# Output projection and feed-forward as 2x2 block products with seven multiplications

## The chip, the core and the metric

The kernel runs on one core of a Trainium2 chip. TensorE multiplies (a stationary operand of 128x128 is loaded, a moving operand of up to 512 columns streams past it, results add up in PSUM banks of 128x512 float32), VectorE and ScalarE work elementwise, GpSimd does little here, and SyncE (SP) issues nearly all DMA. The metric is the device time of one execution in microseconds.

## The reference

One layer of a flow-matching generator over 512 latent tokens of width 2048, with 256 context tokens, in float32. Cut to what matters here:

```python
hx = modulate(rmsnorm(x, norm1_g), sh1, sc1)
q, k, v, g, lf, lb, cb, cc, cx = split_proj(hx @ w_in)
o_x = gla_bidir(...)                       # 4 heads, both directions, from the context's states
y_conv = cb * conv_grid(cc * cx, conv_w)
mix = concat([norm(o_x) * gla_g * silu(g), y_conv]) @ w_out          # [512, 2048] @ [2048, 2048]
x_next = x + gt1 * mix
h2 = modulate(rmsnorm(x_next, norm2_g), sh2, sc2)
x_next = x_next + gt2 * ((silu(h2 @ wg) * (h2 @ wu)) @ wd)           # 2048 -> 2 x 5632 -> 2048
return rmsnorm(x_next, final_g)
```

sh, sc and gt come from `silu(c) @ w_mod + b_mod`.

## The kernel before

Every large product is made from two parts of each operand: `split` casts to a reduced float32 on ScalarE (the high part, L87) and subtracts on VectorE (the low part, L88), and `mm3` adds three matmuls: low x high, high x low, high x high. Activations are kept as [features, tokens]. Weights arrive in units of 128x1024 (512 KB) through four `raw` buffers (`load_w`), and their parts go to three buffers `whi` and three `wlo`. One unit feeds 24 matmuls of 512 columns: its eight 128x128 blocks are the stationary operand, the 512 tokens move, and the result is a tile of 128 features by 512 tokens in one PSUM bank.

The first part projects K, V, q, the gates and the convolution's inputs, and weaves the stages of the attention (`do_gla`) between units of the projections (`weave`). At each step `mod_some` streams 0.7 tiles of the modulation matrix through the same `raw` buffers and reduces each half tile on VectorE (L351): 48 of the 64 tiles run there, 16 beside the first group of the feed-forward.

The output projection then makes 16 tiles of features from the 16 tiles of the mix. The last two go by halves of the tokens, so that the second norm of one half (`row_scale`, `norm2`) runs beside the matmuls of the other. In the feed-forward a group of eight hidden tiles is made (gate `ag` and up `au`, 48 matmuls each; `swiglu`), and then added to all 16 tiles of the output (`acc`, L793); the last group and the final norm go by halves again.

A tile scheduler orders the instructions of each engine ahead of time, by priorities in the order in which the program names them and by its own estimate of when each can run. On the chip every engine works its list off in order, and SP's DMA waits in the same way for free buffers.

Of the kernel before, what the change touches and what calls it, by code (L numbers as in the profile page):

```python
# [13 lines left out]
P = 128  # L14
# [10 lines left out]
NCH = SEQ // CHUNK  # L25
# [3 lines left out]
HT = FFN // P  # L29
EPS = 1e-6  # L30
# [3 lines left out]
# columns of the "cols" input  # L34
C_G1, C_G2, C_FG, C_BMOD, C_GLA, C_CONV = 0, 16, 32, 48, 144, 146
NCOLS = 170
# square constant blocks of the "cst" input
B_ID, B_TRIF, B_TRIB, B_SUFF, B_SUFB, B_MF, B_MB, B_ONE, B_ONE16, B_SELX, B_SELC = range(11)
NBLK = 11
# columns of the "sm" input  # L40
# [5 lines left out]
def tile_hybrid_block(  # L46
    ctx: ExitStack,
    tc: tile.TileContext,
    xT, cT, ccol, crow, cst, sm, cols, gates,
    wsc, wsh, wm2, wk, wv, wl, wq, wg, wc, wo, wfg, wfu, wfd,  # L50
# [7 lines left out]
    xpool = ctx.enter_context(tc.tile_pool(name="xpool", bufs=24))  # L58
    pspool = ctx.enter_context(tc.tile_pool(name="pspool", bufs=1, space=bass.MemoryType.PSUM))

# [29 lines left out]
    def split_scaled(hi, lo, src, scale):  # L90
        """Parts of src * scale, with a scale per partition."""
        nc.scalar.activation(hi, src, AF.Copy, scale=scale)
        nc.vector.scalar_tensor_tensor(lo, src, scale, hi.bitcast(F32), op0=ALU.mult, op1=ALU.subtract)  # L93

    def split_shifted(hi, lo, src, shift):
        """Parts of src + shift, with a shift per partition."""
        nc.scalar.activation(hi, src, AF.Identity, bias=shift)
        nc.vector.scalar_tensor_tensor(lo, src, shift, hi.bitcast(F32), op0=ALU.add, op1=ALU.subtract)  # L98
# [7 lines left out]
    def load_w(src, k, eng=None):  # L106
        """One unit of weights, split into its parts, as [128, k, n]."""
# [14 lines left out]
    def rsqrt_of_sum(pool, s, scale, n):  # L122
        """1 / sqrt(s * scale + eps): square root and reciprocal, then one Newton step."""
# [12 lines left out]
    def row_bcast(ps, pool, r):  # L136
        """ps[m, 128 * tt + t] = r[t, tt] for every m."""
# [6 lines left out]
    cstt = cpool.tile([P, NBLK, P], F32, name="cstt")  # L144
    smt = cpool.tile([P, NSM], F32, name="smt")
    colt = cpool.tile([P, NCOLS], F32, name="colt")
    maskt = cpool.tile([P, 2, SEQ], U8, name="maskt")
    gatet = cpool.tile([33, 2, 512], F32, name="gatet")
    lfT = cpool.tile([33, SEQ + CTX], F32, name="lfT")
# [3 lines left out]
    cbc = cpool.tile([P, D], F32, name="cbc")  # L153
    ident, ones, one16 = cstt[:, B_ID, :], cstt[:, B_ONE, :], cstt[:, B_ONE16, :]
    onecol = cstt[:, B_ONE, 0:1]
# [5 lines left out]
    es_hx = ExitStack()  # L161
    hxpool = es_hx.enter_context(tc.tile_pool(name="hxpool", bufs=1))
# [10 lines left out]
    # Silu of the zeros brings in the table before c is there  # L173
# [3 lines left out]
    def mod_cols(src, c0, n):  # L177
        """silu(c) and silu(c_ctx) times n * 128 columns of w_mod: [128 columns, n, (x, ctx)] in PSUM."""
# [27 lines left out]
    def scaled_chunk(i):  # L206
# [12 lines left out]
        for n, src, acc, dst, pool, q in ((SEQ, xt, saccx, hx, hxpool, 0), (CTX, ct, saccc, hc, hcpool, 1)):  # L219
            hi = pool.tile([P, n], F32R, tag=f"hi{i}", name="hhi")  # L220
            lo = pool.tile([P, n], F32R, tag=f"lo{i}", name="hlo")
# [21 lines left out]

    nc.sync.dma_start(cstt, cst)
# [26 lines left out]
    # ======== V projection of heads 0 and 1 behind the stream of the shift columns ========  # L271
# [6 lines left out]
    def shift_chunk(i):  # L278
        """Chunk i of hx and hc from the scaled rows: norm, then the shift."""
# [21 lines left out]
    def lf_finish(pl, a, n):  # L301
        """Sum of the four partial sums, as rows of lfT."""
# [41 lines left out]
    def mod_some(n, last):  # L344
        """n more of the tiles of 128 features; n may be a fraction."""
# [10 lines left out]

    def mod_finish(a, b):
# [71 lines left out]
    def log_gates(pool, tag, pzs, las):  # L429
        """la = log_sigmoid(z) = min(z, 0) - ln(1 + exp(-|z|)); its 1 / 16 is in the constants."""  # L430
# [8 lines left out]
    def proj_units(acc, wsrc, x, units=(0, 1), part=ALL):  # L439
        """acc = (weight columns)^T x, for one tile of 128 columns; yields after each unit of weights."""  # L440
# [6 lines left out]
    def proj_pair(accs, wsrcs, x, units, part, ws=None, eng=None):  # L447
# [4 lines left out]
        for n, u in enumerate(units):  # L452
            kept = ws is not None and n == 0
            if not kept:
                ws = [load_w(src[u], 8, None if n else eng) for src in wsrcs]
            aw = list(zip(accs, ws))
            for k, (acc, w) in ([(k, a) for a in aw for k in range(8)] if kept else
                                [(k, a) for k in range(8) for a in aw]):
                mm3(acc[:, part], sl(w, ALL, k), sl(x[8 * u + k], ALL, part), n == 0 and k == 0, n == 1 and k == 7)
        return ws  # L460

    def run(*gens):
        for g in gens:
            for _ in g:
                pass

    # ======== context states ========
# [54 lines left out]
    def weave(stages, fill):  # L522
        """A chain's stages between units of the projections, so that TensorE has work while it waits."""
        for _ in stages:
            next(fill, None)
            mod_some(0.7, 48)
        for _ in fill:
            mod_some(0.7, 48)
# [4 lines left out]
    # ======== gated linear attention per head, gated short convolution in between ========  # L533
# [3 lines left out]
    for d in range(2):  # L537
        t = gp.tile([P, SEQ], F32, name=f"msk{d}")
        nc.gpsimd.memset(t, 0.0)
        msk.append(t)  # L540
    las = [[gp.tile([P, 512], F32, name=f"la{d}_{tt}") for tt in range(NX)] for d in range(2)]
# [9 lines left out]
    def do_gla(h):  # L551
        """One head over blocks of 128 tokens; within a block, decays are relative to its middle."""
# [3 lines left out]
        kn = gp.tile([P, 512], F32, tag="kn", name="kn")  # L556
# [3 lines left out]
        for d in range(2):  # L560
# [4 lines left out]
            e = gp.tile([P, 512], F32, tag=f"qe{d}", name="qe")  # L565
            nc.scalar.activation(e, pcm, AF.Exp)
            ke = gp.tile([P, 512], F32, tag="ke", name="ke", bufs=2)
            nc.scalar.activation(ke, pcm, AF.Exp, scale=-1.0)
            # the column of the middle, whose own decay is one, carries the decay from the block's start to it
# [10 lines left out]
            kk = gp.tile([P, 512], F32, tag=f"kd{d}", name="kk")  # L580
# [15 lines left out]
        # o as [tokens, values], two blocks of tokens to a bank  # L596
# [25 lines left out]
        # per-head norm  # L622
# [8 lines left out]
        # back to [values, tokens]; gain and swish gate  # L631
# [35 lines left out]
    mod_some(48, 48)  # L667
    owed[0] = 0.0
    mod_finish(0, 48)
# [3 lines left out]
    es_hx.close()  # L673

    # ======== output projection, gated residual ========
    xnpool = ctx.enter_context(tc.tile_pool(name="xnpool", bufs=1, side="right"))
    mpool = ctx.enter_context(tc.tile_pool(name="mpool", bufs=1))

    def pair(i):
        return (mpool.tile([P, SEQ], F32R, tag=f"hi{i}", name="mhi"),  # L680
                mpool.tile([P, SEQ], F32R, tag=f"lo{i}", name="mlo"))

    order = list(range(8, 16)) + list(range(8))
    mh = [None] * 16
    for i in order:
        mh[i] = pair(i)
        split(*mh[i], mix[i])
    HALF = SEQ // 2
    parts = (slice(0, HALF), slice(HALF, SEQ))
    xn = []  # L690
    sacc = xnpool.tile([P, SEQ], F32, name="sacc")

    def square(m, t, acc):
        """Adds t^2 to acc."""
        s = acc if m == 0 else xnpool.tile([P, SEQ], F32, tag="sqn", name="sqn", bufs=2)[:, : t.shape[-1]]
        nc.scalar.activation(s, t, AF.Square)  # L696
        if m:
            nc.gpsimd.tensor_tensor(acc, acc, s, op=ALU.add)  # L698

    def row_scale(sums):  # L700
        """1 / rms of the rows of one half, the same on every partition; sums: tiles of squares to add up."""
        pms = bank("pms")
        for n, t in enumerate(sums):
            for t2 in range(2):
                mm(pms[:, t2 : t2 + 1], tok(t, t2), onecol, n == 0 and t2 == 0, n == len(sums) - 1)
# [40 lines left out]
    def norm2(hf, rb):  # L746
        part = parts[hf]
        for i in orders[hf]:
            if h2[i] is None:
                h2[i] = pair(i)  # L750
# [181 lines left out]
```

## Time and profile before

| | |
|---|---|
| median of 3 runs | 2482.39 us (2479.9 to 2482.53) |
| span of the profiled execution | 2479.1 us |
| output projection starts at | about 822 us |
| HBM read, written | 329.44 MB, 4.19 MB |
| mean granted TensorE clock | 0.991 |

The span runs from the first to the last instruction of one profiled execution, and is what the stages below are read from; the runs' median is 3.3 us above it. TensorE is busy 98% of the span, but its busy time is modelled and overlapping, so that the number of matmuls and the step from one start to the next tell more than the share.

### The profile page before, as it was taken

Reading aid. Unit: us, or ns where it says so; the run is one execution under the profiler, and the core shown is the slowest. Engines: PE = TensorE matmul, PEld = TensorE weight load, DVE = VectorE, ACT = ScalarE, POOL = GpSimd, SP = SyncE. Lnnn points to the kernel's source line nnn. Section 1 sums busy time; section 2 is a strip of 40 time slices with the busy share of each in tenths; the row PEclk is TensorE's granted clock in tenths of the full one; section 3 lists DMA queues with packets and bytes.
Section 4 is the critical chain, followed back from the end, with each engine's and each line's share of the span. In section 5 each row is a group of like instructions: output and inputs, shape, how many; then the busy total and the mean of one; then the engine's idle time right before and its main releaser. Section 6 shows DMA issues by size and latency. Waiting matters only on the chain.

```text
span 2479.1 us, 27638 instructions
## 1 busy us (share of the span) xinstructions
PE 2420.8 (98%) x11270; PEld 1953.0 (79%) x11270; DVE 1029.9 (42%) x1393; ACT 691.1 (28%) x942; POOL 144.9 (6%) x140
## 2 busy tenths in 40 slices
PE   8999999999999999899999999999999999999997
PEld 5755667787888888788888888888888888888887
DVE  3555155565655533755432233223322232223335
ACT  3522155332323322422212222222122212221232
POOL 2422000000000011300000000000000000000003
PEclk9999999999999999899999999999999999999998
DMA  9763455556553433366433233233322333323231
GB/s 325 231 224 107 161 196 166 177 184 196 187 195 128 161 98 98 112 208 209 125 97 99 94 102 94 95 100 94 101 94 95 101 94 100 96 94 102 94 107 73
DMA packets 117835, 335.45 MB, mean 135 GB/s; under 512 B 12203, under 2 KB 32811, under 8 KB 117580
## 3 DMA queue, kind: packets, MB, share of 16 engines
q1 hardware_dynamic: 117708, 333.69, 41.8%
q8 instruction: 88, 1.44, 0.2%
q14 instruction: 39, 0.32, 0.0%
HBM read 329.44 MB, written 4.19 MB: 135 GB/s over the span
## 4 chain that ended last, share of the span: by engine, by line
PE 78%; DMA 12%; DVE 5%; issue 3%; ACT 2%; SPq 0%; POOL 0%; DVEq 0%; ACTq 0%; POOLq 0%
PE acc L75 41%; PE ag L75 17%; PE au L75 16%; DMA raw<-wm 10%; DVE wlo L88 2%; PE pm L75 1%; DVE raw L351 1%; DMA raw<-wfg 1%; PE pl L75 1%; ACT whi L87 0%; DMA big<-wsh 0%; PE pb L75 0%; DVE mlo L98 0%; PE po L75 0%; DVE big L752 0%
## 5 line engine op out<-in xcount | busy, mean ns | idle before, releaser
L88 DVE TENSOR_TENSOR wlo<-raw,whi 128x1024 fp32r<-128x1024 f32 x386 | 476.3, 1235 | 639.6 <-ACT whi L87 639.4
L87 ACT CAST whi<-raw 128x1024 fp32r<-128x1024 f32 x388 | 407.2, 1051 | 1191.6 <-PE acc L75 558.1
L75 PE MATMUL acc<-big,whi 128*128 128x512 f32 x1280 | 394.0, 389 | 0.0
L75 PE MATMUL ag<-mhi,wlo 128*128 128x512 f32 (+1 forms) x720 | 278.6, 387 | 8.4 <-ACT big L764 6.4
L75 PEld LDWEIGHTS acc<-big,whi 128*128 128x128 f32 x1280 | 240.3, 188 | 49.8
L75 PE MATMUL ag<-mlo,whi 128*128 128x512 f32 (+1 forms) x720 | 277.9, 386 | 0.0
L75 PE MATMUL ag<-mhi,whi 128*128 128x512 f32 (+1 forms) x720 | 277.6, 386 | 0.0
L75 PE MATMUL au<-mhi,wlo 128*128 128x512 f32 (+1 forms) x720 | 277.4, 385 | 0.1
L75 PE MATMUL au<-mlo,whi 128*128 128x512 f32 (+1 forms) x720 | 277.1, 385 | 0.0
L75 PE MATMUL au<-mhi,whi 128*128 128x512 f32 (+1 forms) x720 | 277.0, 385 | 0.0
L75 PE MATMUL acc<-hhi,wlo 128*128 128x512 f32 x640 | 260.7, 408 | 7.0 <-DVE wlo L88 6.2
L75 PE MATMUL acc<-hlo,whi 128*128 128x512 f32 x640 | 252.6, 395 | 0.2 <-DVE hlo L93 0.2
L75 PE MATMUL acc<-hhi,whi 128*128 128x512 f32 x640 | 252.0, 394 | 0.0
L351 DVE CUSTOM_DVE_ANT_0 raw<-raw,cbc 128x1024 f32<-128x1024 f32 x128 | 156.5, 1224 | 228.4 <-DMA raw<-wm 226.1
L75 PE MATMUL acc<-big,wlo 128*128 128x512 f32 x640 | 249.0, 389 | 0.0
L75 PEld LDWEIGHTS ag<-mhi,wlo 128*128 128x128 f32 x720 | 136.5, 190 | 35.7 <-ACT big L764 6.6
L793 DVE SCALAR_TENSOR_TENSOR xn<-acc,modv,xn 128x512 f32<-128x512 f32 x80 | 60.1, 751 | 246.9 <-PE acc L75 246.9
L698 POOL TENSOR_TENSOR sacc<-sacc,sqn 128x256 f32<-128x256 f32 (+1 forms) x41 | 44.2, 1079 | 2017.2 <-ACT sqn L696 2016.8
L75 PEld LDWEIGHTS ag<-mlo,whi 128*128 128x128 f32 x720 | 136.6, 190 | 26.8
L75 PEld LDWEIGHTS au<-mhi,wlo 128*128 128x128 f32 x720 | 135.7, 189 | 27.7 <-DVE wlo L88 1.0
L75 PEld LDWEIGHTS ag<-mhi,whi 128*128 128x128 f32 x720 | 136.4, 189 | 26.7
L75 PEld LDWEIGHTS au<-mlo,whi 128*128 128x128 f32 x720 | 135.7, 188 | 26.8
(202 smaller groups left out, 2768.5 us busy)
## 6 DMA issues: line engine op xcount, KB each, us to landing
raw<-wm SPq DMA_DIRECT2D x128, 512.0 KB, 4.4
raw<-wfg SPq DMA_DIRECT2D x89, 512.0 KB, 3.3
raw<-wfu SPq DMA_DIRECT2D x89, 512.0 KB, 3.3
raw<-wfd SPq DMA_DIRECT2D x80, 512.0 KB, 3.6
raw<-wc SPq DMA_DIRECT2D x48, 512.0 KB, 4.1
raw<-wo SPq DMA_DIRECT2D x34, 512.0 KB, 3.3
big<-wsc SPq DMA_DIRECT2D x64, 256.0 KB, 5.6
big<-wsh SPq DMA_DIRECT2D x64, 256.0 KB, 5.7
```

The source lines that it names most:

```text
L75: nc.tensor.matmul(o, l, r, start=start, stop=stop, skip_group_check=True)
L87: nc.scalar.copy(hi, src)
L88: (eng or nc.vector).tensor_tensor(lo, src, hi, op=ALU.subtract)
L351: nc.vector.tensor_tensor_reduce(out=w, in0=w, in1=cbc[:, hf * 1024 : hf * 1024 + 1024], scale=1.0, scalar=0.0, op0=ALU.mult, op1=ALU.add, ...
L698: nc.gpsimd.tensor_tensor(acc, acc, s, op=ALU.add)
L793: nc.vector.scalar_tensor_tensor(xn[m], acc, modv[:, 48 + m : 49 + m], xn[m], op0=ALU.mult, op1=ALU.add)
```

## The change

The output projection and both halves of the feed-forward become 2x2 block products by Strassen's method in Winograd's form: A is cut by tokens (256 + 256) and by depth, B by depth and by columns (2 x 512), and seven products replace eight. A11, S1 = A21 + A22, S2 = S1 - A11, S4 = A12 - S2, S3 = A11 - A21, A12 and A22 are made once and split (`prep_a`). On the weights' side the sums are made for every call of `seven`: T1 = B12 - B11, T2 = B22 - T1 and T4 = B21 - T2 go through one `ch` buffer per unit, T3 = B22 - B12 through two `raw` buffers. Signs are absorbed, so that every result is a plain sum, taken from PSUM or while copies are added on VectorE.

Now the tokens are stationary and weights move: one unit of 128x1024 (2 depth tiles x 512 columns) feeds 2 x 2 x 3 = 12 matmuls of 512 columns, and the result has 128 tokens on the partitions. `take` adds the residual and sums squares; `norm2` scales rows and transposes 64 blocks on TensorE; `back` transposes the hidden activations (176 blocks) and writes them to DRAM (`actd`), from where the down projection reads them in four groups of 12, 12, 12 and 8 hidden tiles. x passes through DRAM too (`xnd`). All 64 tiles of the modulation are now woven into the first part, 0.95 a step. The pool of 512-column tiles grows from 24 to 72 buffers; the scaled inputs lie in it.

```diff
-    xpool = ctx.enter_context(tc.tile_pool(name="xpool", bufs=24))
+    xpool = ctx.enter_context(tc.tile_pool(name="xpool", bufs=72))
...
+    MOD_STEP = 0.95
...
-            mod_some(0.7, 48)
+            mod_some(MOD_STEP, 64)
...
+    def prep_a(A, pieces):
+        tmp = {}
+        def put(n, i, src):
+            hi, lo = a_unit(A, i, pieces[n][0])
+            split(hi[:, pieces[n][1], :], lo[:, pieces[n][1], :], src)
+        tt = nc.vector.tensor_tensor
+        for n, (u, sel, a11, a12, a21, a22) in enumerate(pieces):
+            put(n, A11, a11())
+        yield
+        for n, (u, sel, a11, a12, a21, a22) in enumerate(pieces):
+            if u not in tmp:
+                tmp[u] = xpool.tile([P, 2, HALF], F32, tag="t", name="s")
+            tt(tmp[u][:, sel, :], a21(), a22(), op=ALU.add)
+            put(n, S1, tmp[u][:, sel, :])
+        yield
...
+    def seven(A, wsrc, nk, after, between=lambda n: None):
+        nu = nk // 2
+        chain = [None] * nu
+        tt = nc.vector.tensor_tensor
...
+        def t2(u):
+            tt(chain[u], raw(3, u), chain[u], op=ALU.subtract)
+            return chain[u]
+        def t3(u):
+            r, r2 = raw(3, u), raw(1, u)
+            tt(r, r, r2, op=ALU.subtract)
+            return r
...
+        plan = (
+            ("u1", A11, b11, X, abank, True), ("v", S1, t1, Y, bank, True), ("u2", S2, t2, X, None, False),
+            ("c12", S4, lambda u: raw(3, u), Y, None, False), ("u3", S3, t3, X, None, False),
+            ("c11", A12, lambda u: raw(2, u), Z, bank, True), ("c21", A22, t4, X, None, False),
+        )
+        for n, (name, i, src, acc, alloc, first) in enumerate(plan):
+            if first:
+                acc += [alloc("acc"), alloc("acc")]
+            for u in range(nu):
+                r = src(u)
+                hi = wpool.tile([P, 1024], F32R, tag="whi", name="whi", bufs=3)
+                lo = wpool.tile([P, 1024], F32R, tag="wlo", name="wlo", bufs=3)
+                split(hi, lo, r)
+                for t in range(2):
+                    for k in range(2):
+                        mm3(acc[t], sl(A[i][u], ALL, k, slice(t * P, t * P + P)),
+                            (hi[:, k * NB : k * NB + NB], lo[:, k * NB : k * NB + NB]),
+                            first and u == 0 and k == 0, u == nu - 1 and k == 1)
+            after[name](acc)
+            between(n)
...
+    def back(j, q):
+        pt = bank("pt")
+        for tt in range(NX):
+            nc.tensor.transpose(tok(pt, tt), acts[j][tt][:, q * P : q * P + P], ident)
+        t = big()
+        nc.scalar.copy(t, pt)
+        nc.sync.dma_start(actd[4 * j + q], t)
...
+        seven(A, lambda b, u: wu[j, b, u], 8, sums(take), between)
...
+    for g, nk in enumerate(GROUPS):
+        A = new_a(nk)
...
+                    nc.sync.dma_start(t, actd[k : k + 2, :, hf * HALF : hf * HALF + HALF].rearrange("k p t -> p k t"))
...
+        for _ in prep_a(A, pieces):
+            pass
+        last = g == len(GROUPS) - 1
...
+        for p in range(NBD // 2):
+            def upd(tt0, c, new):
+                def f(acc):
+                    for t in range(2):
+                        o = y[tt0 + t][2 * p + c]
+                        if g == 0 and new:
+                            nc.scalar.copy(o, acc[t])
+                        else:
+                            nc.vector.tensor_tensor(o, o, acc[t], op=ALU.add)
...
+            seven(A, lambda b, u: wd[w0 + b * (nk // 2) + u], nk, {
+                "u1": upd(0, 0, True), "v": upd(2, 1, True), "u2": upd(0, 1, True), "c12": upd(0, 1, False),
+                "u3": upd(2, 1, False), "c11": upd(0, 0, False), "c21": upd(2, 0, g == 0)})
```

VectorE's list in the feed-forward, before, in the steady part of gate and up (L88 `wlo` is a weight unit's low part, L765 and `big` belong to `swiglu`):

```order
L88 TENSOR_TENSOR wlo<-raw,whi 128x1024
L88 TENSOR_TENSOR big<-big 128x512
L88 TENSOR_TENSOR wlo<-raw,whi 128x1024 x3
L765 TENSOR_TENSOR big<-big,au 128x512
L88 TENSOR_TENSOR wlo<-raw,whi 128x1024
```

The same place now, in the products v and u2 of a call (L97 is the low part, L753 the subtraction of `t2`; one `ch` number is one unit of the chain):

```order
L97 TENSOR_TENSOR wlo_8267<-ch_8177,whi_8266 128x1024
L753 TENSOR_TENSOR ch_8177<-raw_8351,ch_8177 128x1024
L97 TENSOR_TENSOR wlo_8286<-ch_8195,whi_8285 128x1024
L753 TENSOR_TENSOR ch_8195<-raw_8370,ch_8195 128x1024
L97 TENSOR_TENSOR wlo_8305<-ch_8213,whi_8304 128x1024
L753 TENSOR_TENSOR ch_8213<-raw_8389,ch_8213 128x1024
L97 TENSOR_TENSOR wlo_8324<-ch_8231,whi_8323 128x1024
L753 TENSOR_TENSOR ch_8231<-raw_8408,ch_8231 128x1024
L97 TENSOR_TENSOR wlo_8355<-ch_8177,whi_8354 128x1024
```

Between the subtraction of a unit (`ch_8177`) and its low part stand six operations for other units.

SP's list around the product u3 of a call of gate and up (each pair of `raw` in the middle is one unit of T3; `actd` is the store of `back`, which waits for TensorE's transposes and ScalarE's copy):

```order
L112 DMA raw_9663<-wu 128x1024
L112 DMA raw_9681<-wu 128x1024
L915 DMA actd_7392<-big_9536 128x512
L112 DMA raw_9709<-wu 128x1024
L112 DMA raw_9711<-wu 128x1024
L915 DMA actd_7392<-big_9624 128x512
L112 DMA raw_9730<-wu 128x1024
L112 DMA raw_9732<-wu 128x1024
L112 DMA raw_9751<-wu 128x1024
L112 DMA raw_9753<-wu 128x1024
L112 DMA raw_9772<-wu 128x1024
L112 DMA raw_9774<-wu 128x1024
```

Before, SP's list here was two loads for the gate, two for up, and so on, with no store among them. Now eight loads stand in a row for the four units of u3, and stores of the call before stand ahead of some.

VectorE's list at the start of the output projection, behind the last product of the convolution (L650; L707 makes S1, L712 S2; `a0l`, `a1l`, `a2l` are low parts):

```order
L650 TENSOR_TENSOR big<-big,acc 128x512
L97 TENSOR_TENSOR a1l<-s,a1h 128x256 x2
L707 TENSOR_TENSOR s<-big 128x256 x2
L97 TENSOR_TENSOR a0l<-big,a0h 128x256
L97 TENSOR_TENSOR a1l<-s,a1h 128x256 x2
L97 TENSOR_TENSOR a2l<-s,a2h 128x256 x2
L712 TENSOR_TENSOR s<-s,big 128x256 x3
L97 TENSOR_TENSOR a2l<-s,a2h 128x256 x3
L712 TENSOR_TENSOR s<-s,big 128x256 x3
```

Before, 16 low parts of the mix (`mlo`, 128x512) stood there in a row, and then the weights' low parts. Now the small operations go on with S4 and S3 ahead of the first subtraction of weights.

More of the change, by code (lines that the diff above doesn't have):

```diff
@@ L29 @@
 HT = FFN // P
+HALF = SEQ // 2
+NB = 512
+NBD = D // NB
+NPU = FFN // NB
+GROUPS = (6, 6, 6, 4)
 EPS = 1e-6
@@ L445, in proj_units @@
             yield
[L447 to L465, printed above, removed]
     S0 = []
@@ L672, in tile_hybrid_block @@
     es_g.close()
[L673 to L705, printed above, removed]
-        r = rsqrt_of_sum(xnpool, pms[:, :2], 1.0 / D, 2)
-        pr = bank("pr")
-        row_bcast(pr, xnpool, r)
-        t = xnpool.tile([P, HALF], F32, tag="rbc", name="rbc", bufs=2)
-        nc.scalar.copy(t, pr[:, :HALF])
-        return t
@@ L714, in tile_hybrid_block @@
-    NSPLIT = 2
-    pre = []
-    for m in range(KD):
-        pre.append(big())
-        nc.sync.dma_start(pre[m], xT[:, m, :])
-        xn.append(xnpool.tile([P, SEQ], F32, tag=f"xn{m}", name="xn"))
-    def residual(m, acc, part):
-        t = xn[m][:, part]
-        nc.vector.scalar_tensor_tensor(t, acc[:, part], modv[:, m : m + 1], pre[m][:, part], op0=ALU.mult, op1=ALU.add)
-        nc.vector.tensor_scalar(pre[m][:, part], t, gsc2[:, m : m + 1], None, op0=ALU.mult)
-    for m in range(KD - NSPLIT):
-        acc = abank("acc")
-        run(proj_units(acc, wo[m], mh, (1, 0)))
-        residual(m, acc, ALL)
-        square(m, xn[m], sacc)
@@ new lines, in sums, with copied, added, f @@
+    def sums(take):
+        s = {}
+        def copied(name):
+            def f(acc):
+                s[name] = [f2k(name) for _ in range(2)]
+                for t in range(2):
+                    nc.scalar.copy(s[name][t], acc[t])
+            return f
+        def added(name, tt0, c):
+            def f(acc):
+                for t in range(2):
+                    nc.vector.tensor_tensor(s[name][t], s[name][t], acc[t], op=ALU.add)
+                    take(tt0 + t, c, s[name][t], None)
+            return f
+        def direct(acc):
+            for t in range(2):
+                take(2 + t, 0, None, acc[t])
+        return {"u1": copied("u1"), "v": copied("v"), "u2": copied("u2"), "c12": added("u2", 0, 1),
+                "u3": added("v", 2, 1), "c11": added("u1", 0, 0), "c21": direct}
@@ new lines, in cols_to_row, with bcast @@
+    def cols_to_row(a, name):
+        pt = bank("ptr")
+        nc.tensor.transpose(pt[:KD, :P], modv[:, a : a + KD], ident)
+        t = fpool.tile([KD, P], F32, name=name)
+        nc.scalar.copy(t, pt[:KD, :P])
+        row = tc.dram_tile([1, D], F32, name=name + "d")
+        nc.sync.dma_start(row.rearrange("a (k p) -> (a k) p", p=P), t)
+        return row
+    def bcast(row, d):
+        t = big()
+        nc.sync.dma_start(t, row[0, d * NB : d * NB + NB].partition_broadcast(P))
+        return t
@@ new lines, in tile_hybrid_block @@
+    A = new_a(8)
+    norm2(0)
+    rw = lambda hf, u: (lambda: raws[hf, u])
+    gen = prep_a(A, [(u, ALL, rw(0, u), rw(0, 4 + u), rw(1, u), rw(1, 4 + u)) for u in range(4)])
+    next(gen)
+    actd = tc.dram_tile([HT, P, SEQ], F32, name="actd")
+    acts = {}
+    def back(j, q):
+        pt = bank("pt")
+        for tt in range(NX):
+            nc.tensor.transpose(tok(pt, tt), acts[j][tt][:, q * P : q * P + P], ident)
+        t = big()
+        nc.scalar.copy(t, pt)
+        nc.sync.dma_start(actd[4 * j + q], t)
@@ new lines, in tile_hybrid_block, with take, between @@
+    for j in range(NPU):
+        got = acts[j] = [None] * NX
+        ups = {}
+        def take(tt, c, t, acc):
+            if c == 1:
+                ups[tt] = t
+                return
+            if t is None:
+                t = f2k("g21")
+                nc.scalar.activation(t, acc, AF.Silu)
+            else:
+                nc.scalar.activation(t, t, AF.Silu)
+            nc.vector.tensor_tensor(t, t, ups[tt], op=ALU.mult)
+            got[tt] = t
+        def between(n):
+            if j == 0 and n == 0:
+                norm2(1)
+                for _ in gen:
+                    pass
+            if j and n < 4:
+                back(j - 1, n)
+        seven(A, lambda b, u: wu[j, b, u], 8, sums(take), between)
```

339 lines of the change are left out of this document (205 added, 134 removed).

## The prediction

> **What bounds the kernel now.** I read the page's busy shares and chain first, then the busy time by stretches, then single stretches of the timeline.
>
> ```profile
> PE 2420.8 (98%) x11270; PEld 1953.0 (79%) x11270; DVE 1029.9 (42%) x1393; ACT 691.1 (28%) x942; POOL 144.9 (6%) x140
> PE 78%; DMA 12%; DVE 5%; issue 3%; ACT 2%; SPq 0%; POOL 0%; DVEq 0%; ACTq 0%; POOLq 0%
> ```
>
> TensorE carries the chain. The view by stretches (TensorE, its weight loads, VectorE, ScalarE and GpSimd busy with counts, granted clock, DMA share, GB/s) separates the part left almost alone (to 822 us) from the replaced one (822 us to the end):
>
> ```profile
> 338.00:822.00 484.00, 466.64 (x2110) 381.39 (x2109) 266.14 (x430) 169.48 (x253) 0.98 (x2) 0.98 0.55 178
> 976.00:1040.00 64.00, 52.30 (x396) 51.23 (x395) 46.24 (x83) 28.78 (x53) 21.92 (x19) 0.89 0.28 88
> 1040.00:2400.00 1360.00, 1359.90 (x6002) 1125.81 (x6002) 458.89 (x483) 307.80 (x337) 0.00 (x0) 1.00 0.35 109
> 2400.00:2479.10 79.10, 63.12 (x464) 59.77 (x462) 45.47 (x94) 28.26 (x59) 24.34 (x32) 0.91 0.28 97
> 822.00:2479.10 1657.10, 1629.32 (x7543) 1364.63 (x7542) 609.99 (x731) 409.43 (x506) 67.67 (x63) 0.99 0.34 108
> ```
>
> From 1040 to 2400 us TensorE never waits, while VectorE is busy a third of the time and DMA at 109 GB/s. Fewer matmuls shorten this part one for one as long as the others keep up. A busy TensorE is modelled, so I take its pace from starts; the chain in order of time gives it (start us, us, matmuls), and the page gives the group's count:
>
> ```profile
> 1281.05 10.88 PE ag L75 x48
> 1291.93 10.88 PE au L75 x48
> L75 PE MATMUL ag<-mhi,wlo 128*128 128x512 f32 (+1 forms) x720 | 278.6, 387 | 8.4 <-ACT big L764 6.4
> ```
>
> 10.88 / 48 = 0.2267 us for a matmul of 512 columns.
>
> **What is removed.** The plain products need 768 (output projection), 4224 (gate and up: 88 tiles x 16 x 3) and 2112 (down) such matmuls, 7104 in all. Seven products of half the tokens, half the depth and 512 columns need 672 + 3696 + 1848 = 6216. The 888 fewer are worth 888 x 0.2267 = **-201.3 us**. Of the 1657.1 us of the old part, 7104 x 0.2267 = 1610.4 are matmuls. The other 46.7 us (11.7 idle around the second norm, 16.0 idle at the end, half-width matmuls, small sums) go with the old code: **-46.7 us**; what the new code puts there is counted below.
>
> **Pace with tokens stationary.** The V projection of before already works so; its single starts (start us, us):
>
> ```profile
> 246.55 0.40 PE L75 MATMUL acc<-whi,hhi 128*128 128x512 f32 x1
> ...
> 249.33 0.39 PE L75 MATMUL acc<-whi,hhi 128*128 128x512 f32 x1
> ```
>
> Twelve steps in 2.78 us are 0.2317 each, 5 ns more. That stage changes its PSUM bank after 3 matmuls, the feed-forward after 48, the new code after 6. I take the middle, 0.229: 6216 x 0.0023 = **+14 us** (0 to +31).
>
> **Transposes added.** The hidden activations come out with tokens on partitions and are turned back (44 blocks of 4), as is the input of the feed-forward (64). The attention of before shows the price:
>
> ```profile
> 792.11 1.03 PE L635 MATMUL pt<-cstt,on 128*128 128x128 f32 x8
> 792.90 0.48 PE L75 MATMUL acc<-hhi,wlo 128*128 128x512 f32 x1
> 793.21 0.39 PE L75 MATMUL acc<-hlo,whi 128*128 128x512 f32 x1
> ```
>
> Eight take 0.79 us, 0.10 each, and the matmul behind them steps 0.31 instead of 0.23. So 44 x (0.40 + 0.08) + 64 x 0.10 = **+27.5 us**.
>
> **VectorE: additions of weights.** Of the seven products four need a sum of weight blocks, so of seven units of 128x1024 four have an addition besides the cast on ScalarE and the low part on VectorE. Durations, and starts of successive operations:
>
> ```profile
> L88 DVE TENSOR_TENSOR wlo<-raw,whi 128x1024 fp32r<-128x1024 f32 x386 | 476.3, 1235 | 639.6 <-ACT whi L87 639.4
> L87 ACT CAST whi<-raw 128x1024 fp32r<-128x1024 f32 x388 | 407.2, 1051 | 1191.6 <-PE acc L75 558.1 <-PE au L75 329.3 <-issue 198.0
> 682.13 1.22 DVE L88 TENSOR_TENSOR wlo<-raw,whi 128x1024 fp32r<-128x1024 f32 x1
> 683.27 0.16 DVE L127 TENSOR_SCALAR rs_m<-ss 128x4 f32<-128x4 f32 x1
> 821.67 9.11 DVE L88 TENSOR_TENSOR mlo<-big,mhi 128x512 fp32r<-128x512 f32 x15
> 1003.26 0.42 DVE L752 TENSOR_TENSOR big<-big,rbc 128x256 f32<-128x256 f32 x1
> 1003.59 0.48 DVE L98 SCALAR_TENSOR_TENSOR mlo<-big,modv,mhi 128x256 fp32r<-128x256 f32 x1
> ```
>
> An operation of 1024 takes 1.235 but the next starts 1.14 after it; of 512, (9.11 - 0.68) / 14 = 0.60; of 256, 0.33. An addition has the same shape and types as the low part, so I price it alike (it cannot be below its 1.14 without halving the work; above, 1.235). One call of seven products with four units each is 44 x 1.14 + 10 x 0.60 = 56 us of VectorE against 336 x 0.229 = 77 us of TensorE: hidden in the eleven calls of gate and up. In the down projection with three units: 33 x 1.14 + 14 x 0.60 (sums into y) + half of the next group's preparation, 33 x 0.60 / 2 = 10, together 56 against 252 x 0.229 = 57.7. That is no margin for an in-order queue whose sums wait for TensorE. I allow 3 us in each of six calls, 5 us in each of two calls of the last group (22 x 1.14 + 8.4 + 9.6 for the finishing = 43 against 38.5) and 10 us for the first group, whose preparation (33 small operations in one piece) no earlier call hides: **+38 us** (0 if queues stay ahead, 80 if every sum waits a matmul unit of 2.75 us).
>
> [...]
>
> **DMA: eight loads for seven units.** Loads (KB each, us from issue to landing):
>
> ```profile
> raw<-wm SPq DMA_DIRECT2D x128, 512.0 KB, 4.4
> raw<-wfg SPq DMA_DIRECT2D x89, 512.0 KB, 3.3
> ```
>
> A call of gate and up moves 32 x 0.524 MB in 77 us, 218 GB/s; the first slice of the page ran at 325. Tight is the product u3, whose units subtract two loaded blocks: four `raw` buffers are two units, and one pair is busy for 4.4 (landing) + 1.14 + 1.05 + 1.14 + some 0.3 of handing over = 8.0 us, so 4.0 us a unit against 2.75. Two of its four units find their buffers early (the product before frees them one by one), two come 1.3 us late, which the three `wlo` buffers may or may not cover: 2.6 us in 13 calls, **+34 us** (0 to 8 a call, 104).
>
> **Stage borders.** Start of the output projection: the seven sums of the mix are 88 operations of 256 columns. Behind the last convolution's row 64 of them and 16 of the large ones stand ahead of the eleventh weight unit: 64 x 0.34 + 16 x 1.14 = 40 us against 10 x 2.75 = 27.5: **+13 us** (before, 16 splits of 0.60 ran beside the matmuls). Second norm: after the last but one product its chain (three operations on two tiles 3.7, square 0.8, root and small steps 3, scaling 2, transposes and their copies 4, splits 2 = 15.5) has 11 us of cover, 5 stay; the second half's (copies 4, sum, cast, low part 2.3) 6; then the rest of the preparation makes VectorE late by some 6. The border of before, with 11.7 us idle, ran at clock 0.89 over 64 us, 7 us: **+24 us**. End: sums 3.7, square and root 3, eight scalings 5, last store 3.5, **+16 us** (before: 16.0 idle).
>
> ```profile
> 2468.50 6.80 DVE L806 SCALAR_TENSOR_TENSOR big<-xn,colt,rbc 128x256 f32<-128x256 f32 x12 [1.58 <-ACT rbc L710]
> 2470.44 5.22 SPq L808 DMA_DIRECT2D outT<-big  x8
> ```
>
> [...]
>
> **First part.** The 16 tiles of modulation that ran beside the first feed-forward group now run before 822 us, 0.95 instead of 0.7 a step. VectorE there goes from 266 to about 308 of 484 us, and loads from 168 to 200. The chain shows loads on it:
>
> ```profile
> 716.27 5.22 DMA raw<-wm
> 722.88 3.80 DMA raw<-wm
> ```
>
> but TensorE is busy 467 of 484 us. **+5 us** (-5 to +92, below).
>
> **Sum.** -201.3 - 46.7 + 14 + 27.5 + 38 + 34 + 13 + 24 + 16 + 5 = -76.5. The profiled execution spans 2479.1, so 2402.6; the median of the runs is 3.3 above that span: **2406 us**.
>
> **Rivals.** (1) VectorE and the loads keep ahead: the 38 and 34 us fall away, 2406 - 72 = 2334. For it speaks 56 against 77 us in the largest stage, against it the down projection without margin. (2) Slower: VectorE and ScalarE take turns. If the order has addition, cast and low part of one unit in a row, a unit takes 1.14 + 1.05 + 1.14 + 0.2 = 3.5 us against 2.75. There are 74 units per product, 296 with an addition: 296 x 0.75 = 222 in place of my 72, 2556. It decides from (2482 - 2406 + 72) / 296 = 0.5 us exposed for each addition. Against it: in the queue the next unit's addition stands ahead of a unit's low part, so the cast is covered. (3) The first part becomes paced by its loads: 484 / 168 = 2.9 us each, 32 more are 92 us: 2406 - 5 + 92 = 2493, slower. Against it speaks TensorE's 96% there. That the change doesn't remove the matmuls is excluded by the instruction order: 48 of them a product and call.
>
> **How the numbers follow.** Forecast 0.58, (1) 0.17, (2) 0.12, (3) 0.07, others 0.06. The forecast's own range is 2365 to 2455, from the bounds of 34, 38 and 14. For 8 in 10 I reach down to (1) and up to (3): 2335 to 2490. A measurement of this kernel tells 0.2%, 5 us, from no change: faster 0.75 (forecast but its top, (1)), within 0.05, slower 0.20 ((2), (3), and half of the others).
>
> **What would show it.** Right: gate and up take some 80 to 83 us a call, TensorE's waits there name `wlo` of u3 fed by loads, and in the down projection VectorE is busy over 90%. Wrong: waits of TensorE on `wlo` in v and u2 of gate and up (rival 2), a start of the output projection later than 840 us (rival 3), no waits on `wlo` after 1100 us (rival 1), or a matmul step outside 0.226 to 0.232.

## The result

The changed kernel takes 2493.9 us (median of 5 runs, 2487.9 to 2496.3), the kernel before 2482.3 beside it: a ratio of 1.0048, with an interval of 1.0035 to 1.0061. It is slower by half a per cent. The forecast was 2406, with a range up to 2490 and a chance of 0.20 for slower. The profiled execution spans 2492.5 us, so the forecast's sum of 2402.6 missed by 90.

### The profile page after: what moved, and what is told of

Read it like the earlier page. It is cut to its first block, busy times and chain, and to the rows that moved or that the text cites. A ratio compares the mean times of both kernels' runs of the same rounds, so it can differ in the third digit from the quotient of the medians.

```text
span 2492.5 us, 27479 instructions
## 1 busy us (share of the span) xinstructions
PE 2299.3 (92%) x10184; PEld 1806.4 (72%) x10184; DVE 1737.6 (70%) x2140; ACT 1029.4 (41%) x1388; POOL 72.8 (3%) x77
## 5 line engine op out<-in xcount | busy, mean ns | idle before, releaser
L97 DVE TENSOR_TENSOR wlo<-raw,whi 128x1024 fp32r<-128x1024 f32 x318 | 391.0, 1235 | 255.8 <-ACT whi L96 254.7
L96 ACT CAST whi<-ch 128x1024 fp32r<-128x1024 f32 x296 | 310.5, 1050 | 349.7 <-PE acc L84 251.1
L97 DVE TENSOR_TENSOR wlo<-ch,whi 128x1024 fp32r<-128x1024 f32 x296 | 360.3, 1220 | 90.9 <-ACT whi L96 88.5
L84 PE MATMUL acc<-hhi,wlo 128*128 128x512 f32 x640 | 257.7, 410 | 17.6 <-DVE wlo L97 9.5
L84 PEld LDWEIGHTS acc<-hhi,wlo 128*128 128x128 f32 x640 | 122.3, 192 | 49.9 <-ACT hhi L101 9.0
L84 PEld LDWEIGHTS acc<-hlo,whi 128*128 128x128 f32 x640 | 123.6, 193 | 28.3 <-issue 1.9
L84 PEld LDWEIGHTS acc<-hhi,whi 128*128 128x128 f32 x640 | 123.6, 193 | 27.9 <-issue 1.9
L84 PE MATMUL acc<-whi,a0l 128*128 128x512 f32 x296 | 117.5, 398 | 16.2 <-DVE a0l L97 16.2
L84 PE MATMUL acc<-wlo,a1h 128*128 128x512 f32 x296 | 120.6, 407 | 12.4 <-DVE wlo L97 12.4
L84 PE MATMUL acc<-wlo,a6h 128*128 128x512 f32 x296 | 118.7, 401 | 13.3 <-DVE wlo L97 13.3
L84 PE MATMUL acc<-wlo,a4h 128*128 128x512 f32 x296 | 119.1, 402 | 12.7 <-DVE wlo L97 12.5
L84 PE MATMUL acc<-wlo,a0h 128*128 128x512 f32 x296 | 118.0, 399 | 8.1 <-DVE wlo L97 8.1
L758 DVE TENSOR_TENSOR raw<-raw 128x1024 f32<-128x1024 f32 x74 | 90.5, 1223 | 47.7 <-DMA raw<-wu 32.3
L84 PE MATMUL acc<-whi,a1h 128*128 128x512 f32 x296 | 118.9, 402 | 0.0
```

Of the source, the lines that this page charges most:

```text
L84: nc.tensor.matmul(o, l, r, start=start, stop=stop, skip_group_check=True)
L96: nc.scalar.copy(hi, src)
L97: (eng or nc.vector).tensor_tensor(lo, src, hi, op=ALU.subtract)
L758: tt(r, r, r2, op=ALU.subtract)
```

## The profile after, beside the prediction's lines

The page's busy times, TensorE's granted clock in 40 slices, and the chain:

```profile
PE 2299.3 (92%) x10184; PEld 1806.4 (72%) x10184; DVE 1737.6 (70%) x2140; ACT 1029.4 (41%) x1388; POOL 72.8 (3%) x77
PEclk9999999999989999989999999999999989899998
PE 7%; DVE 7%; DMA 3%; issue 1%; ACT 1%; SPq 0%; DVEq 0%; ACTq 0%
```

The chain here reaches back only to 2013 us, a fifth of the span, so its shares tell of the end alone. TensorE is busy 121 us less and was expected to end 77 us earlier; it has 193 us of idle time instead of 58. The view by stretches, cut where the stages of the changed kernel begin (first projections, attention, output projection with the first call of gate and up, the other ten calls, down projection, end):

```profile
0.00:398.00 398.00, 371.79 (x1768) 240.12 (x1769) 176.06 (x271) 131.93 (x212) 72.77 (x77) 0.98 0.61 200
398.00:875.50 477.50, 435.32 (x1963) 359.94 (x1961) 282.52 (x472) 151.98 (x234) 0.00 (x0) 0.95 0.60 195
875.50:1170.60 295.10, 251.95 (x1074) 201.76 (x1073) 250.11 (x339) 153.91 (x239) 0.00 (x0) 0.95 0.63 203
1170.60:1980.60 810.00, 792.02 (x3537) 646.95 (x3535) 590.17 (x546) 371.32 (x427) 0.00 (x0) 1.00 0.70 225
1980.60:2474.90 494.30, 448.20 (x1848) 357.63 (x1848) 426.33 (x490) 218.71 (x273) 0.00 (x0) 0.94 0.65 212
2474.90:2492.50 17.60, 0.03 (x1) 0.00 (x0) 12.44 (x25) 1.54 (x5) 0.00 (x0) 0.63 0.58 207
```

The ten calls of gate and up run as forecast: TensorE busy 792 of 810 us, clock 1.00, 81 us a call. The stages on both sides of them do not. The output projection begins here:

```profile
L84 PE MATMUL acc<-wlo,a0h x296: 389/389/793, 875.8 to 2431.9; 128*128 128x512 f32 x148
```

at 875.5 with its weight load, where the kernel before began at 822. With the start of each product's first matmul taken from the trace, every term of the prediction's sum but the first can be measured: a product of 48 matmuls that waits for nothing takes 10.88 us, and what a product takes beyond that (8.16 for 36, 5.44 for 24) is booked under what held it.

| term (us) | forecast | measured | where |
|---|---|---|---|
| 888 matmuls less, old time between | -248.0 | -248.0 | not measured by itself: the remainder, which closes the sum |
| pace with tokens stationary | +14 | 0 | undisturbed products: 10.88 for 48, as before |
| transposes in the calls | +21.1 | +24.8 | ten calls, 2.5 each |
| second norm with its 64 transposes | +30.4 | +28.5 | last product of the output projection 16.1, next call's first three 12.4 |
| u3 loads | +34 | +32.3 | u3 of the first three calls 16.2, c21 of the first of them 3.8 (gone with six buffers, run 4), ten calls 12.3 (3.0 of it in c11, behind u3) |
| start of the output projection | +13 | +18.0 | its first two products |
| end | +16 | +17.6 | after the last matmul |
| down projection | +38 | **+86.7** | 75.5 in its eight calls, 11.2 at the product ahead of them |
| first part | +5 | **+53.5** | 875.5 - 822 |
| sum | -76.5 | +13.4 | 2479.1 + 13.4 = 2492.5 |

Two terms are wrong by 48.5 and 48.7 us; all others together by 7 the other way. Matmuls into `acc`, counted from the start in both kernels, show where the first part's 53.5 went: the 320th starts at 121.0 us before and at 148.4 now, the 1024th at 376.7 and 398.6 (22 later), the 2560th at 813.0 and 868.1 (55 later). So 22 us are lost while K is projected, a stage of which no computation was changed, and 33 us in the attention.

## Experiments

The runs are numbered in the order in which they were made. Starts and lengths of products are taken from each run's trace; a single time stands beside one run of the kernel before (2476.2 with runs 1 to 4, 2478.3 with 5 to 8, a median of 2481.6 with 9 to 12). The five runs of the changed kernel spread by 8 us, so that differences of a few microseconds between single times say little, and the stages of the traces are compared instead.

### The attention: 16 more modulation tiles (runs 2, 6, 11)

The waits of TensorE in this part, of the kernel before and of the changed one (us, times, longest), and one of VectorE of each:

```profile
PE psc L75 <- DVE qe L574: 6.1, 3, 3.2
PE pt L635 <- ACT on L629: 5.2, 3, 3.0
DVE raw L351 <- DMA raw<-wm: 144.8, 64, 6.0
```

```profile
PE pt L629 <- ACT on L623: 20.3, 3, 8.1
PE psc L84 <- DVE qe L568: 16.4, 6, 4.8
DVE raw L363 <- DMA raw<-wm: 151.5, 78, 4.9
```

TensorE hardly waits for weights (5.5 us for their low parts in the changed kernel), it waits for steps of the attention (`on` is the norm per head, `qe` the decayed queries). VectorE stood almost as long at the modulation's loads before (144.8 us) as it does now (151.5), so its total does not price the loss; what counts is what is queued behind each wait. One such wait in the order of time, on VectorE, ScalarE and VectorE:

```profile
728.76 0.16 DVE L136 TENSOR_SCALAR rs_m<-ss 128x4 f32<-128x4 f32 x1
733.56 1.23 DVE L363 CUSTOM_DVE_ANT_0 raw<-raw,cbc 128x1024 f32<-128x1024 f32 x1 [4.64 <-DMA raw<-wm]
734.71 0.17 DVE L138 RECIPROCAL rs_r<-rs_t 128x4 f32<-128x4 f32 x1
735.77 1.56 ACT L623 ACTIVATE on<-po,rs_r 128x256 f32<-128x256 f32 x4 [6.61 <-DVE rs_r L142]
```

Between the norm's first step and its reciprocal, operations of 0.17 us, stands a modulation reduction whose load has not landed. VectorE stands 4.64 us for it, then works 1.2, and ScalarE (6.61 us, to 735.77) and TensorE (8.08 us, to 736.30) wait behind.

Run 2 puts the 16 tiles into the first part of the kernel *before*:

```
- mod_some(0.7, 48) ... mod_some(2.5, 64) in the first feed-forward group
+ mod_some(0.95, 64), the rest ahead of mod_finish(0, 64), none in the feed-forward
```

> The kernel before, with all 64 modulation tiles ahead of the output projection (0.95 instead of 0.7 a step), none beside the feed-forward. Theory (the 16 tiles make VectorE's queue late for the attention's small steps, about 2 us each tile): the output projection starts near 855 instead of 822 us and, as the feed-forward is bound by TensorE and gains nothing, the span is near 2512. Rival (the shared pool and its order cost the 33 us, the tiles nothing): start at 822 +-5, span 2479 +-5.

2518.1 us. Its attention takes 469.1 us from the 1024th to the 2560th matmul (436.3 before, 469.5 in the changed kernel), and the same waits are there, in the same sizes:

```profile
PE pt L635 <- ACT on L629: 22.3, 3, 8.3
PE psc L75 <- DVE qe L574: 14.6, 5, 3.9
```

So the 33 us belong to the tiles, whatever the rest of the change does. Run 11 takes only their loads away:

```
- w = load_raw(wm2[j][...]);           reduce(out=w, in0=w, in1=cbc[...])
+ w = wpool.tile(..., tag="raw");      reduce(out=w, in0=cbc[...], in1=cbc[...])
```

> The changed kernel with its 64 modulation tiles reduced from data that is already there instead of from loads (the 128 loads of half a megabyte are left out, VectorE's work and the buffers are the same), so the output is not the reference's. Theory (VectorE's queue stands at a reduction until its load has landed, 165 us in all, and the attention's small steps behind it are late): the attention part takes 436 us or less instead of 469.5, span 2460 or less. Rival (the 41 us of VectorE that 32 more reductions take are themselves the delay): 460 us or more, span 2483 to 2493.

2433.2 us; the attention part takes 409.0 us, 27 less than in the kernel before, and the output projection starts 61 us earlier than in the changed kernel,

```profile
L84 PE MATMUL acc<-wlo,a0h x296: 389/389/797, 815.1 to 2371.1; 128*128 128x512 f32 x148
```

and TensorE has no wait left from 395 to 815 us, with all 128 reductions still on VectorE. The busy time of the reductions costs nothing; waiting for their loads costs 61 us, of which the kernel before already paid 27. The run also takes 67 MB out of the DMA queue and frees the `raw` buffers sooner; that the wait in VectorE's list is what counts, and not the traffic, was not tested apart; it is read from TensorE's waits above, which are for steps of the attention, and from run 4, where two more buffers change nothing here (471 us). Run 6 moves the 16 tiles on to gate and up, which were found to have VectorE to spare (busy 590 of 810 us):

```
  front:  mod_some(0.7, 48)                       # was 0.95, 64
+ gate/up, calls 2 to 9: two tiles a call, as 8 reductions of 512 columns
```

> The changed kernel with 48 modulation tiles in the first part (0.7 a step) as before, and the last 16, which only the end needs, two in each of gate and up's calls 2 to 9 (64 more VectorE operations of 512 columns, 5 us a call). Theory (the 16 tiles cost 33 us because VectorE's queue holds the attention's small steps up behind them; gate and up have 20 us of VectorE to spare in a call): the attention part takes 436 instead of 469.5 us, the output projection starts at 843, the eight calls grow by 0 to 1 us, span near 2462. Rival (the cost only moves): these calls take 84 us or more, span 2485 or more.

2496.4 us, no gain. The attention is back at 436 us and the output projection starts at 842.9, as the theory said; but each of the eight calls takes 81 to 85 us, 84 in the mean, where it took 80. The cost moved, as the rival said: over these eight calls TensorE waits 20.2 us for the weights' low parts, where it waited 3.4 us without the tiles, and VectorE stands up to 4.6 us at a late tile's load.

### The K projection: the place of the scaled tokens (runs 1, 5)

Here the change moved the tokens' parts from a pool of their own into the shared pool (72 slots instead of 24). SP's list differs too: weights stand ahead of tokens. Run 1 puts that list back as it was:

```
+ with tc.issue_after(load of the tokens' chunk): load of wk, wv, constants
```

> Only the order of SP's loads is put back: in the K projection every weight unit from the fourth on, the constants and the V projection's weights stand behind the token chunks, as in the kernel before. Theory (the changed load order starves the K projection): the 22 us that this stage lost by 121 us are back, matmul 320 of the projections starts near 121 instead of 148 us, the output projection starts at 853 instead of 875.5, span near 2470. Rival (the pieces of the tokens now live in the shared pool and wait for its slots): the K projection ends as late as in the changed kernel, span 2492 +-5.

2512.1 us, 18 slower than the changed kernel; matmul 320 starts at 167. The theory of the load order fell, and the rival's 2492 was missed as well. TensorE's waits from 20 to 150 us, of the kernel before and of the changed one:

```profile
PE acc L75 <- ACT hhi L92: 0.8, 1, 0.8
```

```profile
PE acc L84 <- ACT hhi L101: 8.1, 7, 1.2
PE pc L84 <- ACT tm L203: 4.3, 8, 0.6
```

TensorE's and its neighbours' rows in the changed kernel show what happens (`pm`, `tm`, `pc`, `gx`, `hhi` are the steps from the modulation's weights to the scaled tokens):

```profile
93.90 0.37 ACT L203 COPY tm<-pm 128x256 f32<-128x256 f32 x1
94.33 0.61 PE L84 MATMUL pc<-smt,tm 128*128 128x2 f32 x4 [0.55 <-ACT tm L203]
95.04 0.46 DVE L219 TENSOR_SCALAR gx<-pc,bsc,colt 128x2 f32<-128x2 f32 x2
95.35 0.72 ACT L101 ACTIVATE hhi<-big,gx 128x512 fp32r<-128x512 f32 x1 [0.54 <-DVE gx L219]
96.12 1.36 PE L84 MATMUL acc<-hhi,wlo 128*128 128x512 f32 x4 [1.19 <-ACT hhi L101]
```

The chain from `tm` to `hhi` stands bare between TensorE's matmuls, once for every two chunks: in TensorE's list `pc` is followed at once by the matmuls that need it. In the list of the kernel before, matmuls of an earlier chunk stand between. Run 5 changes one thing, the slots that the loads can run ahead into:

```
+ for each of the 16 chunks: allocate its parts (3 slots) and clear one column of each, at the start
```

> The changed kernel; the 48 slots of the scaled tokens are taken from the shared pool before the first load (by clearing one column of each), so that 24 slots are left for what comes and goes, as many as the pool of the kernel before had. Nothing else is edited. Theory (in the shared pool the loads run ahead into all 72 slots, and the order that the scheduler then finds puts the scale's products directly ahead of the matmuls that need them): matmul 320 of the projections starts at 121 to 126 instead of 148 us, the output projection at 853, span near 2470. Rival (the pieces' place is not the cause): 148 us or later as in the run with the order of the loads put back, span 2490 or more.

2470.9 us. Matmul 320 starts at 119.6, the output projection at 848.9. The same place in this run:

```profile
96.83 0.50 PE L84 MATMUL pc<-smt,tm 128*128 128x2 f32 x4
97.19 0.48 PE L84 MATMUL acc<-hhi,wlo 128*128 128x512 f32 x1
97.37 0.47 DVE L219 TENSOR_SCALAR gx<-pc,bsc,colt 128x2 f32<-128x2 f32 x2 [5.43 <-PE pc L84]
97.51 0.39 PE L84 MATMUL acc<-hlo,whi 128*128 128x512 f32 x1
```

TensorE works through the chain, and its first 560 matmuls stand again in the order of the kernel before. So the slots free for the loads decided in which order the scheduler put TensorE's matmuls, and that was worth 23 to 27 us; whether by their number or by the claim ahead of the loads, this run does not separate. In run 1 only the loads' order was back, not TensorE's; why it lost another 18 us stays open.

### The down projection: preparation at the borders (runs 3, 7, 9, 10)

At the first border (SP, ScalarE, VectorE, and TensorE's waits from 1970 to 2030 us):

```profile
1972.58 2.13 SPq L915 DMA_DIRECT2D actd<-big  x4
1974.80 7.71 SPq L958 DMA_DIRECT2D ar<-actd  x12
1979.25 0.62 ACT L96 CAST a0h<-ar 128x512 fp32r<-128x512 f32 x1 [5.23 <-DMA ar<-actd]
1979.90 0.69 DVE L97 TENSOR_TENSOR a0l<-ar,a0h 128x512 fp32r<-128x512 f32 x1 [5.96 <-ACT a0h L96]
PE acc L84 <- ACT big L972: 10.0, 1, 10.0
PE acc L84 <- DVE a0l L97: 8.4, 1, 8.4
```

The group's activations are loaded only after the last block of hidden activations has been stored, though the group does not contain that block. TensorE waits 8.4 us for the first part; 10.0 us later on for a copy of results on ScalarE, which stands in its list behind the casts of all seven parts. Run 3 starts each group's loads, sums and parts during the call before:

```
+ def prep_group(g, A): loads of actd[g]; yield; yield from prep_a(A, pieces)
+ seven(..., between=lambda n: next(early, None))     # one stage after each product
```

> The changed kernel, with the sums and parts of a group's activations for the down projection begun during the call before (its loads after that call's first product), the stored activations in one buffer per group. Theory (preparation is not hidden behind earlier calls, it stands alone at the group borders): the some 75 us that TensorE loses at the borders of the down projection shrink to 20, and 1980 us to the end takes 455 instead of 512 us, span near 2435. Rival (VectorE bounds the down projection: it is busy 444 of these 512 us): the work only moves, the part takes 490 us or more, span 2470 or more.

2468.0 us, from the part's first matmul to the end 479.4 us instead of 511.9: a gain of 32 where 57 were expected, between the theory's 455 and the rival's 490. The product v behind the first border falls from 24.1 to 8.2 us, but the second calls of the first two groups, which now hold the preparation of the next group, take 66 to 67 us against 57 of matmuls. Run 9 leaves preparation out to find its price:

```
- for _ in prep_a(A, pieces): pass
+ for _ in prep_a(A, pieces) if g == 0 else (): pass
```

> The changed kernel without the preparation of the second to fourth group in the down projection: these products use the first group's prepared activations, so the output is not the reference's. Theory (the preparation, loads and 33 VectorE operations in one piece at each border, is what the down projection loses): the seven calls after the first, 416 us against 362 of matmuls, fall to 375 us, span near 2452. Rival (the sums of weights and of results fill VectorE's queue): 400 us or more, span 2475 or more.

2462.0 us; the seven calls take 382 us, nearer to the theory's 375 than to the rival's 400. Run 10 leaves out the sums of weights instead:

```
+ if not sums: t1, t2, t3, t4 = (lambda u, b=b: raw(b, u) for b in (1, 3, 3, 2))
```

> The changed kernel without the sums of weight blocks in the down projection: the products v, u2, u3 and c21 take one loaded block each (seven loads instead of eight a unit, 88 VectorE operations of 1024 columns less), so the output is not the reference's. Theory (preparation at the borders is the loss): the 512 us from the part's first matmul to the end fall by 10 to 20 only. Rival (VectorE's queue, 444 us busy of 512, is the loss): they fall by 50 us or more, to 460.

2461.6 us; the part takes 478.6 us, 33 less. The down projection's last seven calls, of the changed kernel, of run 9 and of run 10:

```profile
2058.50:2474.90 416.40, 384.36 (x1597) 307.18 (x1595) 367.64 (x422) 183.12 (x226) 0.00 (x0) 0.95 0.66 218
```

```profile
2061.00:2442.90 381.90, 371.01 (x1597) 302.06 (x1595) 316.93 (x334) 152.71 (x170) 0.00 (x0) 0.98 0.67 216
```

```profile
2055.80:2441.00 385.20, 368.79 (x1597) 302.02 (x1595) 282.41 (x340) 183.40 (x226) 0.00 (x0) 0.98 0.66 208
```

Of 55 us over the 362 of matmuls, 34 go with the preparation and 31 with the sums: together more than the 55, so that they overlap in the queue. Without preparation the five calls ahead of the last group take 57.4 to 59.0 us, so sums of weights and of results alone cost next to nothing there. Without sums the border behind the first group still costs 20 us, and only the one behind the second costs nothing; the last group is different: its two calls, 95.5 us for 76.2 of matmuls, take 92.7 without preparation and 79.0 without sums. There VectorE also finishes the output and is busy 87.7 of 95.4 us, and it is the bound. Neither theory holds for the whole part: borders by preparation, last group by sums. Run 7 tried to lighten the preparation:

```
- yield from prep_a(A, pieces)
+ yield from prep_a(A, pieces, nc.gpsimd.tensor_tensor)
```

> The third run's kernel (preparation of a group begun a call earlier), with the 12 sums of a group's preparation on GpSimd instead of VectorE, 42 operations in all, some 0.60 us each of VectorE. Theory (what is left in the down projection, 461 us to its last matmul against 419 of matmuls, is VectorE, busy 59 of 67 us in a group's second call): the second calls shrink from 67 to 60 us each, the part from 480 to 462 us. Rival (the loads' order or waits on ScalarE hold it): 475 to 485 us; slower GpSimd sums could also make it later.

2472.8 us, no gain over run 3's 2468.0: the second calls take 71.1 and 67.4 us instead of 66.9 and 66.0, the part 489.5 instead of 479.4. The sums that take 0.68 us on VectorE take 1.68 to 2.04 us on GpSimd here, and those of S1, S2 and S4 are links of a chain (S4's row):

```profile
L716 POOL TENSOR_TENSOR s<-ar,s 128x512 f32<-128x512 f32 x8 | 16.3, 2044 | 12.0 <-DVE a2l L97 12.0
```

### u3's loads and the whole (runs 4, 8, 12)

Run 4:

```
- r = wpool.tile([P, 1024], F32, tag="raw", name="raw", bufs=4)      xpool bufs=72
+ r = wpool.tile([P, 1024], F32, tag="raw", name="raw", bufs=6)      xpool bufs=68
```

> Six raw buffers instead of four (and 68 instead of 72 slots in the shared pool to make room). Theory (four buffers pace the pairs of loads of u3 and the modulation tiles in the first part): u3's excess over 10.9 us, 26 us in the 13 calls with four units, falls below 8, the output projection starts some 15 us earlier, span near 2455. Rival (VectorE's queue order, not the buffers, is late): less than 8 us from all, span 2485 to 2495; fewer pool slots could even cost time at the group borders.

2479.9 us. u3 takes 11.0 to 11.6 us in the output projection (16 to 17 with four buffers), 12.9 in the call behind the second norm (15.9), and 11.0 in every other call of gate and up. The theory of the buffers holds for u3: the 32.3 us of the table, c21 of the first call included, fall to some 5 (the product ahead of u3, c12, takes 12.8 instead of 12.0 us in gate and up, so that a call there gains 0.4 only). It does not hold for the attention, 471 us here, and the first projections are 10 us later, likely for the fewer slots, so that the time shrinks by 14 only.

Run 8 joins the slots claimed (5), the late tiles (6) and the early preparation (3):

> All three together: slots claimed, 16 tiles late, preparation a call earlier. Theory (three separate losses of 22, 33 and 26 us): the output projection starts at 822 us, span near 2410, faster than the kernel before by some 2.8%. Rival (the gains overlap or come back as waits on VectorE or SP): span over 2430.

2432.7 us: 62 us of the 81 expected, since the late tiles cost in gate and up what they save ahead of them, as in run 6. Run 12 adds run 4's buffers:

> The eighth run's kernel (slots claimed, 16 tiles late, preparation a call earlier) with six raw buffers and 68 pool slots. Theory (four buffers make the pairs of u3 and the late tiles' loads late: u3 took 16 instead of 11 us in the first three calls, and the eight calls with late tiles 84 instead of 80): 2390 to 2410 us, 3% faster than the kernel before. Rival (VectorE's queue order holds these, and 20 instead of 24 free slots slow the first projections, 10 us in the fourth run): 2425 us or more.

2374.6 us against 2481.6, a ratio of 0.958 with an interval of 0.954 to 0.962, over the same arithmetic as the changed kernel. With six buffers the calls with late tiles take 79.6 to 79.9 us: the tiles cost nothing there, TensorE no longer waits for low parts, and VectorE's longest wait for a late tile's load is 1.6 us instead of 4.6. Its stretches, cut at the same places as above:

```profile
0.00:385.50 385.50, 372.76 (x1776) 236.88 (x1777) 175.76 (x270) 138.83 (x220) 81.40 (x125) 1.00 0.63 210
385.50:821.80 436.30, 423.94 (x1952) 352.71 (x1951) 245.91 (x408) 145.91 (x227) 0.00 (x0) 0.98 0.53 174
821.80:1099.20 277.40, 246.72 (x1075) 199.88 (x1074) 248.77 (x341) 155.44 (x242) 0.00 (x0) 0.96 0.65 219
1099.20:1899.50 800.30, 786.30 (x3531) 647.21 (x3529) 636.30 (x701) 376.32 (x439) 0.00 (x0) 1.00 0.76 249
1899.50:2351.90 452.40, 430.91 (x1857) 348.35 (x1855) 413.39 (x468) 212.79 (x262) 0.00 (x0) 0.99 0.70 230
2351.90:2369.00 17.10, 0.04 (x1) 0.00 (x0) 12.15 (x25) 1.54 (x5) 0.00 (x0) 0.60 0.59 207
```

## Why the prediction was wrong

**The step that failed first is "First part, +5": "but TensorE is busy 467 of 484 us".** The busy share of the stage as it stood was taken for room. It says what the old list left idle, not what 32 more reductions that wait for loads do to small steps queued behind them. For u3 and the down projection the prediction asked what is queued behind a waiting instruction; here it did not. The runs showed 53.5 us in its place, 33 of them by these waits (runs 2, 6 and 11). Rival 3 put the start after 840 us and slower at 2493, which is the time that came; its mechanism is right in kind (loads) and wrong in size (33 us for the tiles, not 92), and the agreement of the totals is chance.

**The K projection had no term at all.** The rest of the first part's loss, 22 us at the 1024th matmul, arose there (run 5). The prediction took the part "left almost alone" as left alone, although the change replaced its pools. The instruction lists of both kernels show the changed order there; the prediction drew only on the lists around the replaced part.

**"Down projection, +38" measured 87.** Its working counted "half of the next group's preparation" in each call, hidden behind matmuls, and 10 us for the first group. At the borders nothing was hidden: at the first, the 12 loads stand in SP's list behind the last stores, the first of them is issued at 1974.8 us, and the first cast starts at 1979.3. The first border alone cost 32 us (11.2 and 20.7, mostly removed by run 3), the second 25. The operations were priced well (0.60 a step of 512 columns); where they stand was not read. The last group's 10 us measured 19, by VectorE, as argued.

**What held.** 10.88 us for a product of 48, so the -201.3; gate and up, forecast at 80 to 83 us a call and measured at 79 to 81 in nine calls and 91 where the next part's border is waited for; transposes, second norm and end within 4 us each. u3's loads: right in mechanism (run 4) and size (32.3 for 34), but spread otherwise, 20.0 in the first three calls, c21 included, and 1.2 in each of the others. The pace's +14 was an allowance for PSUM banks changing; it is 0. VectorE is busy 426 of 494 us in the down projection, 86%, not over 90. Rival 2 (VectorE and ScalarE in turns) did not come: v and u2 of gate and up take 11.4 us, of which the transposes explain 0.5. Two small sums do not come out as written: the end's terms add up to 15.2, not 16, and (2), (3) and half of the others to 0.22, not 0.20; nothing hangs on either.

## What to carry to other kernels

Here the reductions in VectorE's queue, which also carries small steps of a chain, cost 61 us with their loads; with the same operations and without the loads TensorE had no wait left (run 11). Ask of each operation that is added or moved whether its data will be there when its turn comes. Compare the instruction lists of *all* stages whose pools, buffers or tags a change touches, since here the slots that were free reordered a stage whose computation was the same (matmul 320 at 148.4 us, at 119.6 in run 5). And at the first border of the down projection nothing of the preparation was hidden, with its first load issued at 1974.8 us, behind the last stores; with it begun a call earlier the part took 32 us less (run 3). Look for the first load at each border, and for the slots it lands in.

## What was not expected of the hardware

TensorE's half speed came after pauses of less than 2 us too, where the prediction had counted lost clock only at the border with 11.7 us idle. In the changed kernel:

```profile
1030.21 0.73 PE L84 MATMUL acc<-whi,a4l 128*128 128x512 f32 x2 [1.70 <-ACT whi L96]
1032.45 0.79 PE L84 MATMUL acc<-wlo,a4h 128*128 128x512 f32 x1 [1.50 <-DVE wlo L97]
1033.04 0.63 PE L84 MATMUL acc<-whi,a4h 128*128 128x512 f32 x1
...
1035.60 0.44 PE L84 MATMUL acc<-whi,a4l 128*128 128x512 f32 x1
1035.88 0.39 PE L84 MATMUL acc<-wlo,a4h 128*128 128x512 f32 x1
```

Two pauses of 1.70 and 1.50 us, and the next six steps are 0.43 instead of 0.23 us; the granted clock is 0.54 from 1032.4 to 1036.0 us and 1.00 in the 4 us behind. The same follows the bare chain of the K projection, with pauses of 0.55 and 1.19: the clock is 0.50 from 97.0 to 100.4 us, and the steps are 0.43. In the trace's record of the clock, from 20 us to the last matmul, half speed comes in 25 stretches of 3.41, 6.83 or 10.24 us. Counted over the trace, 154 matmuls of 512 columns in these stretches are 0.40 to 0.44 us ahead of the next start (14 in those of the kernel before); at 0.2 us each that is 31 us, against 3, where the prediction had priced 7. It lies within the terms of the table: by this estimate a part of the waits was paid a second time.
